# Two more projections of a decoder layer multiplied as pairs of chunks: the recurrent branch's input and the second half of the last gate

## The chip, the cores and the metric

The kernel runs on one core of a Trainium2 chip. The metric is the device time of one execution in microseconds (us); several executions give a median. A profiled execution gives the trace, on which the span runs from the first instruction to the last. The engines are named as in the profile: PE multiplies matrices (PEld loads its stationary operand), DVE is the vector engine, ACT the scalar engine, POOL is GpSimd, SP issues most of the transfers.

## The reference, cut to what matters

One decoder layer for 256 tokens of width 2048 in float32. One wide projection feeds three branches, each of 1024 channels: block attention (A), sliding-window attention (B), and a convolution with a gated linear recurrence (C). The layer ends in an output projection and a per-layer gate.

```python
h = rmsnorm(x, norm_g)
proj = h @ w_in                      # split into qa, ka, va, ga, qb, kb, vb, gb, xc, gc, mg
ya = moba_attention(qa, ka, va, ...)
yb = swa_attention(qb, kb, vb, ...)
yc = rglru_branch(xc, ...)
y_d = einsum(stack([ya * silu(ga), yb * silu(gb), yc * silu(gc)]), w_br)
merged = sum of sigmoid(mg) * y_d over the three branches
x = x + merged @ w_out
x = x + sigmoid(rmsnorm(x, ple_norm_g) @ w_pg) * (p @ w_pp)
return rmsnorm(x, final_norm_g)
```

Two products matter here: xc, which is h times a 2048 x 1024 slice of w_in, and x times w_pg, the last gate (2048 x 2048), of which the second 1024 columns are changed.

## The kernel before, in words

**Float32 from three products.** A float32 operand is split into a high part (an ACT copy with rounding, L141, or L139 where the sign is turned) and the remainder (a DVE subtraction, L147 or L145). `mm3` (L194) multiplies high by high, high by low and low by high into the same PSUM bank. A weight tile is 128 x 1024, two blocks of 512 columns. It is fetched by SP into one of six raw buffers (`fetch`, L104), split into one of four pairs of split buffers (`split`, L120), and then feeds 12 matmuls: two k-tiles, two halves of 128 tokens, three products. The splits are emitted 100 places ahead in priority (LEAD).

**Chunks and pairs.** A chunk is 512 output columns over 16 k-tiles: `project` (L228) runs it in eight weight tiles. `pair_of` (L264) computes two chunks together. For the first four k-tiles it treats tokens, k-tiles and chunks as 2 x 2 blocks and forms the result from seven block products (named `seven`, `one`, `six`, `five`, `three`, `two`, `four`) instead of eight; each is 6 matmuls on a weight tile of its own. The operand sums on the activation side come from `make_sums` (L248), once for each input; those on the weight side are tiles called `chain` and `lone` in a block `b_...`. SP loads a row of weights into each (L391) and POOL adds another row on top in an accumulating transfer (L275); further terms are added in the same way or on DVE, which the argument `adds` chooses. Four products, the heads, are queued in `coming` and run between the weight tiles of whatever comes before the pair; `head` (L204) decides when, counting the tiles that are left. Their partial sums z are copied out of PSUM, summed and, for chunk 0, placed as the start of the pair's own PSUM tile, on which everything else accumulates. `rest` (L359) then runs the remaining twelve k-tiles, six tiles for each chunk, with `three`, `two` and `four` after turns 0, 2 and 4. With `inside` set, the heads accumulate in the pair's own PSUM tile; there are two such tiles of two banks and four single banks (`aux`).

**Order of the work.** PE works through the projections in the order of the code: va (two chunks), xc (two chunks), then the pairs gc, qa, ka, ga and so on. A tile scheduler orders the instructions of every engine by priority and by data. What is not matrix work is paced by hand: at each weight tile a `tick` (L155) pops one step from the lists `side` and `todo`, and timers set with `later` run after a number of ticks. Branch C's gates are such steps (`gates_of`, L729, four for each of eight blocks); the scan and what follows are popped from `side` while ka and ga are computed (L1033). The operand sums of h are made while the first chunk of xc is multiplied (hook at k-tile 8, L783).

A result chunk is turned to feature order (`to_features`, L697): ACT scales it out of PSUM, DVE transposes 32 x 32 blocks, and SP writes it to HBM and reads it back (`flip`, L870), four transfers and one. Ten ticks later (`SETTLE`) `place` (L765) copies it to where the convolution reads it.

**The last gate.** Its chunks 0 and 1 are interleaved (L1217) so that the last four k-tiles, whose input comes last, are multiplied at the end. Chunk 2 follows as one chunk. Chunk 3 is run in three passes over weights that are kept: 48 matmuls of 512 columns for tokens 0 to 127, then two passes of 48 with 256 columns each for the other tokens, so that little work is left behind the last matmul. Each piece goes through `output` (L1181): sigmoid, times the parked product, plus x, square sum, and a multiplication by the final weights (L1188); `store` scales by the final norm and writes out.

There are 14 blocks of 128 x 2048 (`block`), and four buffers of 128 x 1024 for short use (`temp`).

Of the kernel before, what the change touches and what calls it, by code (L numbers as in the profile page):

```python
# [16 lines left out]
P = 128  # L17
# [31 lines left out]
SETTLE = 10  # L49
RV = 384  # L50
# [4 lines left out]
def trunk(ctx: ExitStack, tc: tile.TileContext, x, early, table, onehot, maskv, w_in, sinks, conv, w_ri, vec, fin, w_br,  # L55
# [138 lines left out]
    def mm3(ps, a, b, first, last, **more):  # L194
        (ah, al), (bh, bl) = a, b
        nc.tensor.matmul(ps, ah, bh, start=first, stop=False, **more)  # L196
        nc.tensor.matmul(ps, ah, bl, start=False, stop=False, **more)  # L197
        nc.tensor.matmul(ps, al, bh, start=False, stop=last, **more)  # L198
# [65 lines left out]
    def pair_of(act, sums, src, row, name, inside=False, adds=4, early=1):  # L264
# [29 lines left out]
        def product(n, a, r, dst, start=False, stop=False):  # L294
            w = split(f"{name}_m{n}", r, n == 1)
            for q in range(2):
                mm3(dst, a(q), [t[:, q * CW : (q + 1) * CW] for t in w], q == 0 and start, q == 1 and stop,
                    skip_group_check=True)
# [41 lines left out]
        def two():  # L340
            pss.append(matrix_psum(f"{name}_1"))
            for h in range(NH):
                place(pss[1][:, h], z[h])
            r = raw_of(3)
            with tc.issue_after(banks[1]):
                product(2, whole(1, 0), r, pss[1][:, 0])
# [3 lines left out]
        def four():  # L350
            product(4, whole(1, 1), chain, pss[1][:, 1])
            tick()
# [6 lines left out]
        def rest(ends, done, at_turn=(0, 2, 4), then=None):  # L359
# [4 lines left out]
            def usual(i, k0):  # L364
# [5 lines left out]
                for k in range(k0, k0 + WT // CW):  # L370
                    c = slice((k - k0) * CW, (k - k0 + 1) * CW)
                    for h in range(NH):
                        mm3(pss[i][:, h], [t[:, h * P : (h + 1) * P] for t in act()[k]], [t[:, c] for t in w], False,
                            k == KD - 1, skip_group_check=True)

            turns = [(i, k) for a, b in zip((PAIRED,) + ends, ends) for i in range(2) for k in range(a, b, WT // CW)]
            for n, (i, k) in enumerate(turns):
# [6 lines left out]
                if then is not None and n == THEN:  # L384
                    then()

# [210 lines left out]
    def in_pair(before, inside=False, early=1, adds=4):  # L597
        r = row_no[0] + before * KD * CW // WT
        coming, rest = pair_of(lambda: h_act, lambda: sums["h"], w_in, r, f"in{r}", inside, adds, early)

        def finish(done, then=None):
# [82 lines left out]
    first_ps = in_chunk(hooks={14: tables})  # L684
    works = [lambda c=c: squares(c) for c in range(4)] + [norm_rows, bias_rows]
    second_ps = in_chunk(hooks={2 * i: f for i, f in enumerate(works)})
# [37 lines left out]
    def branch_c():  # L724
# [36 lines left out]
        def turned_xc(c, ps):  # L761
# [9 lines left out]

            later(SETTLE, place)

# [14 lines left out]
        gs = [temp(f"gc{c}").rearrange("p k t -> p (k t)") for c in range(2)]  # L788
        gc_pair(lambda c, ps: to_features(gs[c], ps, rs1, f"gc{c}"), qa[0][0])
# [36 lines left out]
        steps += [(lambda c: split_act(z, 4 * c, 4, flipped(gs[c], 8), "zc"), c) for c in range(2)]  # L826
# [43 lines left out]
    def flip(dst, srcs, n, name, queue=nc.sync):  # L870
# [9 lines left out]
        queue.dma_start(dst, d)  # L880
# [145 lines left out]
    def branch_a(rest, qa_pair):  # L1026
# [3 lines left out]
        def turned_k(c, ps):  # L1030
            to_features(chunk(kT, c), ps, rs1, f"ka{c}")
            if c == 0:
                side.extend([lambda: None] * 4 + rest)  # L1033
# [32 lines left out]
    def turn_later(u, n, src, name, gain=None, ticks=TURN_LATE):  # L1066
# [15 lines left out]
        if n == 0 and name == "m":  # L1082
            later(ticks + 1, lambda: sums_of(u, name))
# [89 lines left out]
    for n, (to, src) in enumerate(rows):  # L1173
        later(2 + n, lambda to=to, src=src: nc.scalar.dma_start(to, src))
# [34 lines left out]

    def gated(n, ps):  # L1210
# [5 lines left out]
    gets = [weights_of(w_pg, i * KD * CW // WT, f"pg{i}", WT // CW) for i in range(2)]  # L1216
    for last in (False, True):  # L1217
# [9 lines left out]
    gated(2, project(act_of(*x2T), w_pg, 2 * KD * CW // WT, "pg2"))  # L1227

    kept.update(f"pg3_{s}" for s in range(KD // 4))
    ws = weights_of(w_pg, 3 * KD * CW // WT, "pg3", WT // CW)  # L1230
    y, junk = token_major(temp("y3")), token_major(temp("jz3"))
    c0 = 3 * CW
    ps = project(act_of(*x2T), None, 0, "pg3", weights=ws, half=0)
    output(0, c0, CW, ps, y[:, 0, :], junk[:, 0, :], square_act(0, 3))()
# [4 lines left out]
    def part_of(c):  # L1239
        def get(k):  # L1240
            w, kk = ws(k)
            return [t[:, kk * CW + c * HW : kk * CW + (c + 1) * HW] for t in w], 0
        return get

    for c in range(2):
        ps = project(act_of(*x2T), None, 0, f"pg{3 + c}", cw=HW, weights=part_of(c), half=1)[:, :HW]
# [31 lines left out]
def _pack_pair(w, ends=(KD,)):  # L1278
# [3 lines left out]
    for lo, hi in zip((PAIRED,) + ends, ends):  # L1282
        for t in (a, b):
# [4 lines left out]
def _columns_of(w, paired):  # L1288
    parts, at = [], 0
    for width, pair in paired:  # L1290
        c = w[:, at : at + width]
        at += width
        parts += [_pack_pair(c[:, i : i + 2 * CW]) for i in range(0, width, 2 * CW)] if pair else [_pack(c)]
# [64 lines left out]
```

## Time and profile before

| | |
|---|---|
| median of 3 runs | 979.05 us (978.0 to 981.14) |
| the profiled execution's own time | 977.16 us |
| its span | 975.1 us |
| matmuls | 4390, PE busy 965.5 us |
| DVE, ACT busy | 721.8 us, 620.9 us |
| transfers | 255.71 MB, mean 262 GB/s |

How to read the rows: a row of the timeline has the start in us from the span's start, the duration in us, the engine (a q behind it is its queue, which issues transfers), the line of the code, the operation, output<-inputs, the shape, and in brackets the idle time before it and what ended it. A row of a group has busy us and mean ns of one behind the bar. PE's matmuls overlap, so the distance between two starts tells more than a duration.

### The profile page before, as it was taken

The numbers are of one execution on the slowest core, as the hardware profiler recorded it, in microseconds if no ns is written. First come the engines' busy times: TensorE is split into PE (matmuls) and PEld (weight loads), VectorE is DVE, ScalarE is ACT, GpSimd is POOL, SyncE is SP. The second block draws the span as 40 slices with busy tenths as digits, with TensorE's granted clock in tenths as the row PEclk, the third lists the DMA queues.
The fourth block names the chain that finished last, engine by engine and source line by source line (L and its number), as shares of the span: only waits on it lengthen the run. The fifth ranks groups of instructions, "written<-read, shape, count | busy, mean of one in ns | idle before, by whom it ended". The sixth has DMA issues, their size and how long they took to land.

```text
span 975.1 us, 12612 instructions
## 1 busy us (share of the span) xinstructions
PE 965.5 (99%) x4390; PEld 804.3 (82%) x4390; DVE 721.8 (74%) x1005; ACT 620.9 (64%) x881; POOL 33.1 (3%) x45
## 2 busy tenths in 40 slices
PE   9999999999999999999999999999999999999996
PEld 7888888888888888888888888888888888888886
DVE  6855898866897676667677788788578587765673
ACT  7654776667777666556566866765566565665652
POOL 0010000010000000000000000000000000000000
PEclk9999999999999999999999999999999999999999
DMA  9978989799989865897787876776978998788742
GB/s 342 352 236 253 328 270 340 249 308 281 305 266 321 257 219 189 249 280 244 237 282 245 286 230 225 231 227 208 303 203 280 301 297 305 254 278 334 233 151 87
DMA packets 90264, 255.71 MB, mean 262 GB/s; under 512 B 10152, under 2 KB 31704, under 8 KB 90072
## 3 DMA queue, kind: packets, MB, share of 16 engines
q1 hardware_dynamic: 72720, 216.69, 64.4%
q0 software_dynamic: 4752, 17.30, 9.8%
q10 hardware_dynamic: 12728, 20.91, 6.4%
q8 instruction: 34, 0.56, 0.2%
q14 instruction: 30, 0.25, 0.1%
HBM read 234.13 MB, written 20.75 MB: 261 GB/s over the span
## 4 chain that ended last, share of the span: by engine, by line
PE 98%; DMA 0%; DVE 0%; ACT 0%; SPq 0%; issue 0%; DVEq 0%; ACTq 0%
PE ps_in L197 21%; PE ps_in L196 20%; PE ps_in L198 20%; PE ps_pg L198 3%; PE ps_pg L196 3%; PE ps_pg L197 3%; PE ps_out L196 3%; PE ps_out L198 3%; PE ps_out L197 3%; PE ps_bra L197 1%; PE ps_bra L196 1%; PE ps_brc L197 1%; PE ps_brc L198 1%; PE ps_brc L196 1%; PE ps_brb L197 1%; PE ps_brb L196 1%
## 5 line engine op out<-in xcount | busy, mean ns | idle before, releaser
L147 DVE TENSOR_TENSOR wl_in<-r_in,wh_in 128x1024 fp32r<-128x1024 f32 x196 | 239.0, 1222 | 95.6 <-ACT wh_in L141 91.3
L197 PE MATMUL ps_in<-wl_in,h 128*128 128x512 f32 x784 | 305.6, 390 | 0.4 <-DVE wl_in L147 0.4
L196 PE MATMUL ps_in<-wh_in,h 128*128 128x512 f32 x784 | 305.6, 390 | 0.0
L198 PE MATMUL ps_in<-wh_in,h 128*128 128x512 f32 x784 | 305.3, 389 | 0.0
L141 ACT CAST wh_in<-r_in 128x1024 fp32r<-128x1024 f32 x196 | 205.3, 1051 | 141.3 <-PE ps_in L198 105.1
L197 PEld LDWEIGHTS ps_in<-wl_in,h 128*128 128x128 f32 x784 | 147.3, 188 | 30.4 <-DVE wl_in L147 0.8
L198 PEld LDWEIGHTS ps_in<-wh_in,h 128*128 128x128 f32 x784 | 147.2, 188 | 30.4
L196 PEld LDWEIGHTS ps_in<-wh_in,h 128*128 128x128 f32 x784 | 147.2, 188 | 30.0
L147 DVE TENSOR_TENSOR wl_in_m<-b_in,wh_in_m 128x1024 fp32r<-128x1024 f32 x36 | 43.9, 1220 | 22.7 <-ACT wh_in_m L141 22.2
L147 DVE TENSOR_TENSOR wl_pg<-r_pg,wh_pg 128x1024 fp32r<-128x1024 f32 x28 | 33.9, 1222 | 27.4 <-ACT wh_pg L141 26.6
L141 ACT CAST wh_in_m<-b_in 128x1024 fp32r<-128x1024 f32 x36 | 37.8, 1049 | 25.0 <-PE ps_in L198 13.1
L275 POOL DMA_DIRECT2D b_in<-w_in_dram x29 | 25.5, 878 | 638.6 <-DMA b_in<-w_in_dram 395.7
L196 PE MATMUL ps_pg<-wh_pg,x_hi 128*128 128x512 f32 (+1 forms) x120 | 45.0, 375 | 0.0
L197 PE MATMUL ps_pg<-wl_pg,x_hi 128*128 128x512 f32 (+1 forms) x120 | 45.0, 375 | 0.0
L198 PE MATMUL ps_pg<-wh_pg,x_lo 128*128 128x512 f32 (+1 forms) x120 | 45.0, 375 | 0.0
L141 ACT CAST wh_pg<-r_pg 128x1024 fp32r<-128x1024 f32 x28 | 29.1, 1049 | 22.1 <-PE ps_pg L198 17.3
L196 PE MATMUL ps_out<-wh_out,m_hi 128*128 128x512 f32 x96 | 37.3, 389 | 0.0
L197 PE MATMUL ps_out<-wl_out,m_hi 128*128 128x512 f32 x96 | 37.3, 389 | 0.0
L198 PE MATMUL ps_out<-wh_out,m_lo 128*128 128x512 f32 x96 | 37.3, 389 | 0.0
L147 DVE TENSOR_TENSOR wl_out<-r_out,wh_out 128x1024 fp32r<-128x1024 f32 x24 | 29.1, 1220 | 10.2 <-ACT wh_out L141 10.2
L141 ACT CAST wh_out<-r_out 128x1024 fp32r<-128x1024 f32 x24 | 25.2, 1050 | 12.5 <-PE ps_out L198 8.1
L141 ACT CAST wh_brb<-r_brb 128x1024 fp32r<-128x1024 f32 x16 | 16.9, 1053 | 20.6 <-PE ps_brb L198 10.9
(360 smaller groups left out, 1638.3 us busy)
## 6 DMA issues: line engine op xcount, KB each, us to landing
r_in<-w_in_dram SPq DMA_DIRECT2D x223, 512.0 KB, 4.9
r_pg<-w_pg_dram SPq DMA_DIRECT2D x32, 512.0 KB, 4.8
r_out<-w_out_dram SPq DMA_DIRECT2D x30, 512.0 KB, 5.0
b_in<-w_in_dram POOLq DMA_DIRECT2D x29, 512.0 KB, 8.4
b_in<-w_in_dram SPq DMA_DIRECT2D x18, 512.0 KB, 5.3
r_brc<-w_br_dram SPq DMA_DIRECT2D x16, 512.0 KB, 6.3
r_bra<-w_br_dram SPq DMA_DIRECT2D x16, 512.0 KB, 4.3
r_brb<-w_br_dram SPq DMA_DIRECT2D x16, 512.0 KB, 6.3
```

The lines of the kernel that those rows point to most:

```text
L141: casts.append(nc.scalar.copy(hi[:, c], r[:, c]).ins)
L147: los.append(nc.vector.tensor_tensor(lo[:, c], r[:, c], of, op=ALU.subtract).ins)
L196: nc.tensor.matmul(ps, ah, bh, start=first, stop=False, **more)
L197: nc.tensor.matmul(ps, ah, bl, start=False, stop=False, **more)
L198: nc.tensor.matmul(ps, al, bh, start=False, stop=last, **more)
L275: nc.gpsimd.dma_start(t, src[row + i], accum_op=ALU.add)
```

## The change

1. *xc becomes a pair* with a new order (`late`): its second chunk is multiplied first. Its PSUM tiles start from the ordinary k-tiles; the partial sums z are added to them in PSUM by DVE at the end of each chunk (`finish`). The seven products are run at turns 2, 3, 4, 5, 7, 8 and 9 of its twelve (`XC_AT`). It is opened at k-tile 9 of the second chunk of va, and the sums of h are made at k-tile 12 of that chunk.
2. *The pair gc* is opened at turn 6 of xc and no longer runs its heads in its own PSUM tile; the pair qa is prepared at turn 11. The steps behind get other distances: `place` after 13 ticks instead of 10, two more empty steps ahead of the scan's list, three ahead of each part of the result's split.
3. *Chunks 2 and 3 of the last gate become a pair* (`parts`), opened while chunk 0 is multiplied; its heads run between the tiles of chunks 0 and 1. Chunk 3's part of the first four k-tiles is placed in three single banks (half 0, and two of 256 columns), and product `four` is split into two of 256 columns. The three passes then cover the remaining twelve k-tiles. The sums of that input are made twelve ticks after its first quarter is there.
4. The parked products and final weights are loaded from tick 10 on instead of 2. The multiplications by the final weights for chunks 0 to 2 move into chunk 3's first pass (`weighing`).

The weights are packed in the order that this needs. The core of the diff:

```diff
+SUMS_LATE = 12
+PARKED_LATE = 10
+OPEN_AT = (0, 8)
+XC_AT = (2, 3, 4, 5, 7, 8, 9)
...
         def five():
             product(5, sum_of(0), lone, banks[0], stop=True)
             place(z[2], banks[0])
+            if late:
+                z[3] = lone[:, CW:]
+                banks[1] = on_vector(z[3], z[2], banks[7], ALU.add)
+                return
             if not inside:
...
         def two():
-            pss.append(matrix_psum(f"{name}_1"))
-            for h in range(NH):
-                place(pss[1][:, h], z[h])
+            if parts:
+                pss.append([aux(f"ps_{name}_{c}") for c in range(3)])
+                place(pss[1][0], z[0])
+                for c, t in enumerate(pss[1][1:]):
+                    place(t[:, :QW], z[1][:, c * QW : (c + 1) * QW])
+            elif not late:
+                pss.append(matrix_psum(f"{name}_1"))
+                for h in range(NH):
+                    place(pss[1][:, h], z[h])
...
+        def turned_over(usual, done, then):
+            pss[:] = [None, matrix_psum(f"{name}_1")]
+            turns = [(i, k) for i in (1, 0) for k in range(PAIRED, KD, WT // CW)]
+            steps = heads[:4] + [three, two, four]
+
+            def finish(i):
+                for h in range(NH):
+                    on_vector(pss[i][:, h], pss[i][:, h], z[2 * (1 - i) + h], ALU.add)
+                done(i, pss[i])
+
+            for n, (i, k) in enumerate(turns):
+                if n == KD // 4 + 2:
+                    pss[0] = matrix_psum(f"{name}_0")
+                if i == 0:
+                    head(len(turns) - n)
+                for _ in range(late.count(n)):
+                    steps.pop(0)()
+                usual(i, k)
+                if not steps and n == late[-1]:
+                    finish(1)
+                if n in then:
+                    then[n]()
+            finish(0)
...
+    def prepare_xc():
+        xc_pair.append(in_pair(0, adds=2, late=XC_AT)[1])
+
-    second_ps = in_chunk(hooks={2 * i: f for i, f in enumerate(works)})
+    second_ps = in_chunk(hooks={2 * i: f for i, f in enumerate(works)} | {9: prepare_xc, 12: sum_h})
...
-            later(SETTLE, place)
+            later(SETTLE + 3, place)
...
-        for c in range(2):
-            if c:
-                open_gc, gc_pair = in_pair(1, True)
-                open_gc()
-            turned_xc(c, in_chunk(hooks={14: prepare} if c else {8: sum_h}))
+        def prepare_gc():
+            gc.append(in_pair(0))
+            gc[0][0]()
+
+        xc_pair[0](turned_xc, {6: prepare_gc, 11: prepare})
+        gc_pair = gc[0][1]
...
-        later(2 + n, lambda to=to, src=src: nc.scalar.dma_start(to, src))
+        later(PARKED_LATE + n, lambda to=to, src=src: nc.scalar.dma_start(to, src))
...
-            output(h, n * CW, CW, ps[:, h, :], y[:, h, :], junk[:, h, :], square_act(h, n))()
+            weighing.append(output(h, n * CW, CW, ps[:, h, :], y[:, h, :], junk[:, h, :], square_act(h, n)))
...
+                if (i, k) == OPEN_AT:
+                    open_pair, pair = pair_of(lambda: act_of(*x2T), lambda: sums["x2"], w_pg, row, "pg2", early=0, parts=True)
+                    open_pair()
+                if (i, k) in ((1, KD - 6), (0, KD - 4), (0, KD - 2), (1, KD - 4)):
+                    coming.pop(0)()
...
-    gated(2, project(act_of(*x2T), w_pg, 2 * KD * CW // WT, "pg2"))
+    pss = pair((KD,), lambda i, ps: gated(2, ps), chunks=range(1))
...
+    def products(at, h, c, n):
+        for k in range(KD - PAIRED):
+            w, kk = ws(k)
+            if weighing and n == CW and kk:
+                weighing.pop(0)()
+            ends[at] = mm3(pss[1][at][:, :n], [t[:, h * P : (h + 1) * P] for t in act_of(*x2T)[PAIRED + k]],
+                [t[:, kk * CW + c : kk * CW + c + n] for t in w], False, k == KD - PAIRED - 1, skip_group_check=True)
+        return pss[1][at][:, :n]
```

More of the change, by code (lines that the diff above doesn't have):

```diff
@@ L197, in mm3 @@
         nc.tensor.matmul(ps, ah, bl, start=False, stop=False, **more)
-        nc.tensor.matmul(ps, al, bh, start=False, stop=last, **more)
+        return nc.tensor.matmul(ps, al, bh, start=False, stop=last, **more).ins
     coming = []
@@ L262, in make_sums, with pair_of @@
         return parts
-    def pair_of(act, sums, src, row, name, inside=False, adds=4, early=1):
+    def pair_of(act, sums, src, row, name, inside=False, adds=4, early=1, parts=False, late=()):
         names = ("11", "12", "22", "21")
@@ L350, in four @@
         def four():
-            product(4, whole(1, 1), chain, pss[1][:, 1])
+            if parts:
+                product(4, whole(1, 1), chain, [t[:, :QW] for t in pss[1][1:]])
+            else:
+                product(4, whole(1, 1), chain, pss[1][:, 1])
             tick()
@@ L357, in pair_of, with rest @@
         heads = [seven, one, six, five] + [settle] * early
-        def rest(ends, done, at_turn=(0, 2, 4), then=None):
+        def turned_over(usual, done, then):
[19 more added lines that the diff above has]
+            finish(0)
+        def rest(ends, done, at_turn=(0, 2, 4), then=None, chunks=range(2)):
             while coming and coming[0] in heads:
@@ L372, in usual @@
                     for h in range(NH):
-                        mm3(pss[i][:, h], [t[:, h * P : (h + 1) * P] for t in act()[k]], [t[:, c] for t in w], False,
-                            k == KD - 1, skip_group_check=True)
-            turns = [(i, k) for a, b in zip((PAIRED,) + ends, ends) for i in range(2) for k in range(a, b, WT // CW)]
+                        mm3(pss[i][:, h], [t[:, h * P : (h + 1) * P] for t in act()[k]], [t[:, c] for t in w],
+                            bool(late) and k == PAIRED, k == KD - 1, skip_group_check=True)
+            if late:
+                return turned_over(usual, done, then)
+            turns = [(i, k) for a, b in zip((PAIRED,) + ends, ends) for i in chunks for k in range(a, b, WT // CW)]
             for n, (i, k) in enumerate(turns):
@@ L595, in trunk, with in_pair, finish @@
     sums = {}
-    def in_pair(before, inside=False, early=1, adds=4):
+    def in_pair(before, inside=False, early=1, adds=4, late=()):
         r = row_no[0] + before * KD * CW // WT
-        coming, rest = pair_of(lambda: h_act, lambda: sums["h"], w_in, r, f"in{r}", inside, adds, early)
-        def finish(done, then=None):
+        coming, rest = pair_of(lambda: h_act, lambda: sums["h"], w_in, r, f"in{r}", inside, adds, early, late=late)
+        def finish(done, then={} if late else None):
             row_no[0] += 2 * KD * CW // WT
@@ L1032, in turned_k @@
             if c == 0:
[L1033 removed]
+                side.extend([lambda: None] * 6 + rest)
         following.pop(0)(turned_k, begin_next)
@@ L1081, in turn_later @@
         later(ticks, finish)
-        if n == 0 and name == "m":
-            later(ticks + 1, lambda: sums_of(u, name))
+        if n == 0:
+            later(ticks + (1 if name == "m" else SUMS_LATE), lambda: sums_of(u, name))
     def merge(z, bi, br):
@@ L1292, in _columns_of @@
         at += width
-        parts += [_pack_pair(c[:, i : i + 2 * CW]) for i in range(0, width, 2 * CW)] if pair else [_pack(c)]
+        parts += [_pack_pair(c[:, i : i + 2 * CW], late=pair > 1) for i in range(0, width, 2 * CW)] if pair else [_pack(c)]
     return np.concatenate(parts)
```

60 lines of the change are left out of this document (38 added, 22 removed).

## The prediction

> **What bounds the kernel now.** I read the page first: its busy shares, its slices and its chain.
>
> ```profile
> span 975.1 us, 12612 instructions
> PE 965.5 (99%) x4390; PEld 804.3 (82%) x4390; DVE 721.8 (74%) x1005; ACT 620.9 (64%) x881; POOL 33.1 (3%) x45
> ...
> PE   9999999999999999999999999999999999999996
> DVE  6855898866897676667677788788578587765673
> ...
> PE 98%; DMA 0%; DVE 0%; ACT 0%; SPq 0%; issue 0%; DVEq 0%; ACTq 0%
> ```
>
> The chain that ended last is 98% matmuls, and no slice but the last shows PE under 9 tenths. So a matmul less is worth its pitch, as long as nothing new makes PE wait; everything on another engine is free until then. The pitch is not the 389 ns that one matmul lasts, because they overlap. The timeline of PE gives it, from first and last rows:
>
> ```profile
> 61.65 0.39 PE L196 MATMUL ps_in<-wh_in,h 128*128 128x512 f32 x1
> 83.41 0.39 PE L196 MATMUL ps_in<-wh_in,h 128*128 128x512 f32 x1
> ...
> 88.84 0.39 PE L196 MATMUL m_in<-wh_in_m,sum_h 128*128 128x512 f32 x1
> 90.20 0.39 PE L196 MATMUL ps_in<-wh_in,h 128*128 128x512 f32 x1
> ...
> 955.35 0.28 PE L196 MATMUL ps_pg<-wk_pg,x_hi 128*128 128x256 f32 x1
> 961.10 0.28 PE L196 MATMUL ps_pg<-wk_pg,x_hi 128*128 128x256 f32 x1
> ```
>
> The first chunk of the recurrent projection is 96 matmuls from 61.65 to 83.41: 226.7 ns each, 2.72 us for a weight tile of 12. A product of a pair is 6 matmuls in 1.36 us, the same pitch. A half pass of the last gate, with 256 columns, is 48 matmuls in 5.75 us: 119.8 ns each.
>
> How near the other engines are to making PE wait is read in the busy time by stretch (columns: window, its length, then PE, PEld, DVE, ACT, POOL, the clock, the DMA share, GB/s) and in the timeline of ACT and DVE:
>
> ```profile
> 61.00:108.00 47.00, 47.00 (x209) 38.93 (x208) 28.63 (x29) 26.00 (x31) 3.96 (x5) 1.00 0.92 282
> 108.00:150.00 42.00, 42.00 (x195) 35.03 (x194) 36.72 (x76) 29.93 (x44) 3.20 (x4) 1.00 0.94 294
> 193.00:236.00 43.00, 43.00 (x195) 35.75 (x194) 29.05 (x29) 27.24 (x34) 3.49 (x4) 1.00 0.94 291
> 236.00:278.00 42.00, 42.00 (x187) 34.78 (x186) 36.12 (x37) 34.57 (x40) 3.47 (x4) 1.00 0.97 301
> 889.00:911.00 22.00, 22.00 (x99) 18.22 (x98) 12.51 (x13) 12.48 (x15) 0.71 (x1) 1.00 0.88 333
> ...
> 80.89 1.05 ACT L141 CAST wh_in_m<-b_in 128x1024 fp32r<-128x1024 f32 x1 [1.67 <-PE ps_in L198]
> ...
> 283.38 1.22 DVE L147 TENSOR_TENSOR wl_in<-r_in,wh_in 128x1024 fp32r<-128x1024 f32 x1
> 284.52 1.22 DVE L416 TENSOR_TENSOR zc_lo<-gc,zc_hi 128x1024 fp32r<-128x1024 f32 x1
> 285.65 1.22 DVE L147 TENSOR_TENSOR wl_in_m<-r_in,wh_in_m 128x1024 fp32r<-128x1024 f32 x1
> ```
>
> The cast at 80.89 feeds the product whose first matmul is the row at 88.84: 7.95 us ahead, and it had waited 1.67 us for PE to free one of the four split buffers. In this stage the splits are as far ahead as the buffers let them be. DVE is 61% busy there, 87% in the next stretch and back to back near 284, yet PE is busy the whole of each stretch: DVE at 87% has been carried without a stall.
>
> **The change, part by part.** *Fewer matmuls.* The recurrent projection (xc) has 2 chunks x 16 k-tiles x 2 halves x 3 = 192 matmuls. As a pair it has 7 products x 6 = 42, and 2 x 12 x 2 x 3 = 144 for the other twelve k-tiles: 186. Six less at 226.7 ns: **-1.36 us**. The last two chunks of the gate have 96 + 48 matmuls of 512 columns and 96 of 256. Afterwards there are 36 for six products, 72 for the third chunk's rest and 36 for half 0: again 144 of 512; and 12 for product four plus 72 in the two half passes: 84 of 256. Twelve less at 119.8 ns: **-1.44 us**. Together **-2.80 us**, all on the path.
>
> On this the Trainium skill (TensorE: Matmul & The Clock Gate, Back-to-back issue gap) has columns/2.4 + 2.5 ns for a warm matmul, 216 and 109 ns here, by which the sum would be 2.60 us (an estimate from that page); the rows, 226.7 and 119.8, decide.
>
> *More splits and sums beside them.* Each new pair splits three more weight tiles and adds these:
>
> ```profile
> L147 DVE TENSOR_TENSOR wl_in<-r_in,wh_in 128x1024 fp32r<-128x1024 f32 x196 | 239.0, 1222 | 95.6 <-ACT wh_in L141 91.3
> L141 ACT CAST wh_in<-r_in 128x1024 fp32r<-128x1024 f32 x196 | 205.3, 1051 | 141.3 <-PE ps_in L198 105.1
> L279 DVE TENSOR_TENSOR b_in<-b_in,r_in 128x1024 f32<-128x1024 f32 x7 | 8.6, 1223 | 3.4 <-DMA r_in<-w_in_dram 3.3
> L279 DVE TENSOR_TENSOR ps_in<-b_in,m_in 128x512 f32<-128x512 f32 x9 | 6.2, 694 | 2.5 <-ACT b_in L284 2.1 <-ACT ps_in L284 0.4
> L284 ACT COPY ps_in<-z_in 128x512 f32<-128x512 f32 x18 | 10.6, 589 | 0.3
> L875 DVE STREAM_TRANSPOSE flip_qa<-qa 128x1024 f32<-128x1024 f32 x2 | 2.5, 1246 | 0.0
> 84.56 1.26 ACT L702 ACTIVATE xc<-ps_in,rs_in 128x512 f32<-128x512 f32 x2
> ```
>
> For xc on DVE: 3 x 1.22, two chain sums of 1.22, a subtraction and an addition of 0.69, the four closing sums in PSUM at 0.69, and one transpose of 1.25 that lay in the next stage: 3.66 + 2.44 + 1.38 + 2.76 + 1.25 = 11.5 us, so 28.6 + 11.5 = 40.1 of 47 us, 85%. That is below the 87% that the next stretch carries. The dense place is turns 7 to 9, where three products of xc and four of its neighbour (gc) share three turns: 7 x 1.36 + 3 x 2.72 = 17.7 us of PE against ten splits (12.2), one chain sum, one subtraction and two closing sums, 15.5 us of DVE. It fits, with 2 us over; the tightest split is that of turn 7, with 3 x 1.36 us between the freeing of its buffer and its use, less 2.3 for cast and remainder: 1.8 us of slack. Cost zero; 1.5 us if DVE comes there with the whole of another transpose and chain sum in front.
>
> *The closing sums.* gc is no longer computed inside its own PSUM tile, because xc holds both; its sum has to wait until chunk 1 of xc is read out. After xc's product four that is 2 x 0.69 on DVE, 1.26 on ACT, a copy of 0.59 and a sum of 0.69: 3.9 us, against the turns 9, 10 and 11 of PE, 8.2 us. Zero; queued behind are only splits, which have 1.8 us or more.
>
> *Loads and queues.* A pair's chain is a load from SP and an accumulating one from POOL on top:
>
> ```profile
> b_in<-w_in_dram POOLq DMA_DIRECT2D x29, 512.0 KB, 8.4
> b_in<-w_in_dram SPq DMA_DIRECT2D x18, 512.0 KB, 5.3
> ...
> 41.92 1.06 ACT L141 CAST wh_in<-r_in 128x1024 fp32r<-128x1024 f32 x1 [0.71 <-PE ps_in L198]
> 54.06 1.64 POOL L450 TENSOR_TENSOR rs_in<-rs_in,half_c 128x2 f32<-128x2 f32 x1 [44.33 <-DVE rs_in L449]
> 64.61 0.91 SPq L391 DMA_DIRECT2D b_in<-w_in_dram  x2
> 101.98 0.91 SPq L391 DMA_DIRECT2D b_in<-w_in_dram  x2
> ```
>
> With the split (2.3 us) a chain needs 5.3 + 8.4 + 2.3 = 16.0 us before its first matmul. xc's is opened behind the cast at 41.92, so at about 43; its first matmul is two turns after 61.65, near 67: 24 us. On POOL the two accumulating loads come ahead of the row at 54.06; they wait for loads that land near 49, so it isn't held. gc's chain, now at 64.61, 24 us before 88.84, is opened at xc's turn 6, one turn before use; but SP fetches six raw tiles ahead. The fetch in front of it stands level with turn 1, and from there to gc's first product are 6 x 2.72 + 4 x 1.36 = 21.8 us of PE, and the split lead on top. Zero, as long as that holds (second rival). The two transposed copies of xc come near each other on SP, which the fetch-ahead covers.
>
> *What moves later.* The steps of the recurrent gates start some 25 us later and so run into 193 to 236, where DVE is 68% busy; two of eight blocks, about 7 us of DVE, make it 84%. Zero. In the last gate, the operand sums (some 4 us of DVE) and three splits fall where DVE is 57% busy (889 to 911). The loads that move ten ticks back still go out several tiles before they are read. Zero.
>
> *The tail.* Six multiplications by the final weights move into the last full pass, now 36 x 226.7 ns = 8.2 us.
>
> ```profile
> L1188 DVE TENSOR_TENSOR xr<-xr,fg 128x512 f32<-128x512 f32 (+1 forms) x8 | 5.0, 654 | 1.6 <-ACT jz L1191 1.6
> 955.55 0.69 ACT L1184 ACTIVATE y<-ps_pg,rs 128x512 f32<-128x512 f32 x1 [3.80 <-PE ps_pg L198]
> 963.05 0.19 ACT L1191 ACTIVATION_READ_ACCUMULATOR jz<-xr 128x1 f32 x1
> 967.06 0.47 ACT L1184 ACTIVATE y<-ps_pg,rs 128x256 f32<-128x256 f32 x1 [3.82 <-PE ps_pg L198]
> ```
>
> That is 4.1 us, beside four steps of 0.69 for the third chunk and one or two splits: 8.1 to 9.3 us. From half 0 (955.55) to the end of the first half pass (963.05, and some 0.9 on DVE) the side work takes 8.4 us; the two half passes leave it 11.5 now and 72 x 119.8 ns = 8.6 afterwards. So zero to 0.6 us; I take zero, since the first four multiplications need nothing of that pass.
>
> The sum against the profiled execution's own time is 977.16 - 2.80 = 974.4 us. It lay 1.9 us under the median of 979.05, so in terms of the median: **976.3 us**.
>
> **Rivals.** *First: DVE is crowded.* For it: splits with little slack at turn 7 and back-to-back work near 284, where the steps now end two ticks later. Against: the stretches at 87% without a stall. Its price is 1.5 us at turn 7, or the 0.6 of the tail, or both: 977.0 to 978.4, say 977.7, no measurable difference.
>
> *Second, slower: gc's chain comes late.* If SP sends its loads only when turn 6 is split, as those at 101.98 sit behind a cast, they go out 7.95 + 2.72 = 10.7 us ahead of gc's first product where 16.0 are needed. PE waits 5.3 us there. The load that is then accumulated on the same chain for product six (8.4, and 2.3 for its split) starts with no lead left, 10.7 us against the 3 x 1.36 + 2.72 = 6.8 us of PE between the two products, so PE waits another 3.9 us, and the kernel ends at 976.3 + 9.2 = 985.5 us. It decides from the point where the lead falls below 16.0 us, and the gain is gone when 2.8 us are waited. For it: with xc's own, all 14 blocks of the pool are taken, and a late release holds the loads. Against: this opening stands in no hook and depends on a fetch alone. The same delay would come if accumulating loads took longer:
>
> ```profile
> L275 POOL DMA_DIRECT2D b_in<-w_in_dram x29: 865/868/1046, 69.4 to 718.9; - x29
> ```
>
> Minimum, median and maximum of an issue lie within 0.2 us, whatever DVE does. The Trainium skill (DMA: Bandwidth & Descriptors, SWDGE vs HWDGE vs iDMA) says that DVE in its two-port mode locks GpSimd out of the descriptor rings, which speaks against more such loads; these 29 issues show no sign of it.
>
> **How the numbers follow.** About 0.3%, 2.9 us, is what can be told from no change here. My sum of 2.8 lies just inside, and a median of such runs moves by half a microsecond to one (three of them spread from 978.0 to 981.14). Forecast, 0.72: 976.3, give or take 1.2 for the two medians, 975.1 to 977.5; the bound of 976.1 cuts it a little below its middle, so 0.35 of it lies beyond the bound and 0.37 within. Crowded DVE, 0.17: 0.15 within it and 0.01 beyond either end by the spread of the medians. Late chain, 0.11: slower. So faster 0.36, same 0.52, slower 0.12. The range takes in the forecast with both ends of its median and the crowded case with both its prices; the late chain is left out: 974.8 to 979.0.
>
> **What would show it.** PE with 4372 matmuls instead of 4390; no PE row with idle time before it near 86 (gc's first product), at turn 7, or where gc begins; the cast of gc's first product waiting for PE and not for b_in; the last half passes 36 matmuls each, the first step of the third output 8.6 us after half 0's. A PE row that waits for wl or b_in there, or a last slice that grows, proves me wrong.

## The result, and the profile after

The changed kernel takes **985.09 us** (median of 6 runs, 983.52 to 986.79) where the kernel before took 978.35 (6 runs, 977.19 to 981.14): ratio 1.0064, 95% interval 1.0049 to 1.008. It is slower by about 6.7 us where 2.8 less were forecast, and the time lies outside the forecast's range of 974.8 to 979.0. The profiled execution took 985.03 us.

First the page of the changed kernel:

```profile
span 983.2 us, 12645 instructions
PE 966.3 (98%) x4372; PEld 802.7 (82%) x4372; DVE 738.2 (75%) x1027; ACT 631.9 (64%) x899; POOL 37.6 (4%) x51
...
PE   9999999999999999999999999999999999999896
...
PEclk9999999999999999999999999999999999999898
...
PE 5%; DMA 1%; DVE 0%; ACT 0%; issue 0%; DVEq 0%; ACTq 0%
```

The 18 matmuls are gone (4372), and ahead of the tail one slice of PE falls under 9 tenths, the third from the end (910 to 934), where the clock does so too. The chain that ended last was 98% PE before; now it can be followed back only to a transfer that was issued at 911.55, through some 7% of the span. The account starts from there.

Where the time lies is read from PE's first rows of each stage. At the first row of the gate (878.59, before 879.19) the changed kernel is 0.60 us ahead. From there to the end of the last matmul it takes 96.17 us where it took 87.83 and should take 1.44 less, 86.39. The tail behind the last matmul grew from 8.10 to 8.49. So 8.3 us were lost inside the last gate. PE's rows there show two places:

```profile
900.12 0.39 PE L203 MATMUL ps_pg<-wh_pg,x_lo 128*128 128x512 f32 x1
902.09 0.49 PE L201 MATMUL ps_pg<-wh_pg,x_hi 128*128 128x512 f32 x1 [1.59 <-ACT wh_pg L146]
903.35 0.50 PE L202 MATMUL ps_pg<-wl_pg,x_hi 128*128 128x512 f32 x1 [0.76 <-DVE wl_pg L152]
...
919.45 0.39 PE L203 MATMUL ps_pg<-wh_pg,x_lo 128*128 128x512 f32 x1
923.76 0.79 PE L201 MATMUL ps_pg<-wh_pg,x_hi 128*128 128x512 f32 x1 [3.92 <-ACT wh_pg L146]
924.35 0.70 PE L201 MATMUL m_pg<-wh_pg_m,sum_x 128*128 128x512 f32 x1
```

From start to start, less the pitch of 0.23: the first wait is 1.75 + 1.03 + 0.11 = 2.9 us, the second 4.08 + 0.36 + 0.27 = 4.7 us. Behind the second, some ten matmuls come 427 ns apart instead of 227, another 2.0 us; from 925.0 to 929.3 the granted clock was 0.52. Together 9.6 us, of the 96.17 - 86.39 = 9.8 to be explained. Both waits are for ACT's cast of an ordinary weight tile, so the next view is ACT's timeline, with its queue, of the changed kernel:

```profile
887.50 2.20 ACTq L942 DMA_DIRECT2D d_x<-flip_x  x2
889.80 2.00 ACT L146 CAST wh_pg<-r_pg 128x1024 fp32r<-128x1024 f32 x2 [1.27 <-PE ps_pg L203]
900.53 0.34 ACTq L946 DMA_DIRECT2D turn_x<-d_x  x1
901.00 1.99 ACT L146 CAST wh_pg<-r_pg 128x1024 fp32r<-128x1024 f32 x2 [9.20 <-DMA r_pg<-w_pg_dram]
...
908.46 1.04 ACT L146 CAST wh_pg_m<-b_pg 128x1024 fp32r<-128x1024 f32 x1
...
921.72 1.04 ACT L146 CAST wh_pg_m<-b_pg 128x1024 fp32r<-128x1024 f32 x1 [8.94 <-DMA fg<-fin_dram]
922.67 1.04 ACT L146 CAST wh_pg<-r_pg 128x1024 fp32r<-128x1024 f32 x1
```

and the same in the kernel before:

```profile
888.75 1.34 ACTq L879 DMA_DIRECT2D d_x<-flip_x  x2
890.13 0.48 ACTq L1174 DMA_DIRECT2D fg<-fin_dram  x1
...
895.60 0.33 ACTq L880 DMA_DIRECT2D turn_x<-d_x  x1
896.05 2.00 ACT L141 CAST wh_pg<-r_pg 128x1024 fp32r<-128x1024 f32 x2 [3.03 <-PE ps_pg L198]
```

ACT issues the four writes of the transposed copy (d_x) and then the read back (turn_x), which waits for them. That shows in the landing of the last write: in the changed kernel it came 12.2 us after the issue at 888.25, and the read back went out 0.1 us later; in the kernel before 5.9 us after the issue at 889.57, and again the read back 0.1 us later. ACT takes its work in order: while its queue stands at the read back, no split behind it starts (here the cast comes 0.47 us behind it, in the third experiment and both probes below 0.46 or 0.47). From the end of the last write's issue to the read back 5.5 us passed before (890.09 to 895.60) and 10.8 us after (889.70 to 900.53). In both kernels ACT made two more splits in that time; then it was idle for 3.0 us before and 9.2 us after. The idle time in brackets names the load of r_pg. That load was no cause: the cast's tile, asked for at 881.99, had landed by 887.53 by the trace's semaphore counts. The second hole ends with product six's cast (921.72); the ordinary tile's cast is queued behind it. The chain of waits of the changed kernel names the releaser:

```profile
911.55 10.07 DMA b_pg<-w_pg_dram
...
922.67 1.05 ACT wh_pg L146
923.72 0.04 issue
923.76 0.79 PE ps_pg L201
```

This is the accumulating load that adds to the tile `chain` between product seven, cast at 908.46, and product six. (The brackets at 921.72 name the load of fg, which nothing there reads.)

The engine time and the traffic around the first hole, before and after (columns as in the prediction: the last two are the DMA share and GB/s):

```profile
884.00:902.00 18.00, 18.00 (x81) 14.92 (x80) 12.35 (x14) 8.49 (x11) 0.71 (x1) 1.00 1.00 388
```

```profile
884.00:902.00 18.00, 16.51 (x73) 13.33 (x71) 9.36 (x13) 6.34 (x10) 2.43 (x3) 1.00 0.92 281
888.00:892.00 4.00, 4.00 (x20) 3.30 (x19) 2.35 (x2) 2.53 (x3) 0.68 (x1) 1.00 0.97 217
```

In 888 to 892, while the four writes run, the DMA engines are busy at 0.97 but move 217 GB/s. The kernel before moves 341 at a share of 0.93 in the same four us, and 388 at 1.00 over the 18 us. The two accumulating loads that open the gate's pair were issued just ahead, by POOL:

```profile
885.61 0.86 POOL L280 DMA_DIRECT2D b_pg<-w_pg_dram  x1 [102.80 <-DVE wl_pg L152]
886.89 0.86 POOL L280 DMA_DIRECT2D b_pg<-w_pg_dram  x1 [0.42 <-issue]
```

### The profile page after: what moved, and what is told of

Its sections match the earlier page's. It is cut to its first block, busy times and chain, and to the rows that moved or that the text cites. A ratio compares the mean times of both kernels' runs of the same rounds, so it can differ in the third digit from the quotient of the medians.

```text
span 983.2 us, 12645 instructions
## 1 busy us (share of the span) xinstructions
PE 966.3 (98%) x4372; PEld 802.7 (82%) x4372; DVE 738.2 (75%) x1027; ACT 631.9 (64%) x899; POOL 37.6 (4%) x51
## 5 line engine op out<-in xcount | busy, mean ns | idle before, releaser
L202 PE MATMUL ps_in<-wl_in,h 128*128 128x512 f32 x768 | 299.7, 390 | 0.4 <-DVE wl_in L152 0.4
L201 PE MATMUL ps_in<-wh_in,h 128*128 128x512 f32 x768 | 299.4, 390 | 0.0
L203 PE MATMUL ps_in<-wh_in,h 128*128 128x512 f32 x768 | 299.3, 390 | 0.0
L152 DVE TENSOR_TENSOR wl_in<-r_in,wh_in 128x1024 fp32r<-128x1024 f32 x192 | 233.8, 1220 | 87.0 <-ACT wh_in L146 83.7
L146 ACT CAST wh_in<-r_in 128x1024 fp32r<-128x1024 f32 x192 | 201.2, 1051 | 136.0 <-PE ps_in L203 110.0
L202 PEld LDWEIGHTS ps_in<-wl_in,h 128*128 128x128 f32 x768 | 144.2, 188 | 30.1 <-DVE wl_in L152 0.8
L203 PEld LDWEIGHTS ps_in<-wh_in,h 128*128 128x128 f32 x768 | 144.2, 188 | 29.8
L201 PEld LDWEIGHTS ps_in<-wh_in,h 128*128 128x128 f32 x768 | 144.2, 188 | 29.6
L152 DVE TENSOR_TENSOR wl_in_m<-b_in,wh_in_m 128x1024 fp32r<-128x1024 f32 x40 | 48.8, 1221 | 24.4 <-ACT wh_in_m L146 23.7
L146 ACT CAST wh_in_m<-b_in 128x1024 fp32r<-128x1024 f32 x40 | 42.0, 1050 | 26.9 <-PE ps_in L203 17.6
L152 DVE TENSOR_TENSOR wl_pg<-r_pg,wh_pg 128x1024 fp32r<-128x1024 f32 x26 | 31.5, 1220 | 24.3 <-ACT wh_pg L146 24.3
L203 PE MATMUL ps_pg<-wh_pg,x_lo 128*128 128x512 f32 (+1 forms) x112 | 42.3, 378 | 0.0
```

The lines of the kernel that those rows point to most:

```text
L146: casts.append(nc.scalar.copy(hi[:, c], r[:, c]).ins)
L152: los.append(nc.vector.tensor_tensor(lo[:, c], r[:, c], of, op=ALU.subtract).ins)
L203: return nc.tensor.matmul(ps, al, bh, start=False, stop=last, **more).ins
```

## The experiments

**Theory one** is read from these rows: the accumulating loads of the gate's pair do the harm. The two that open it run on top of the transposed copy and hold ACT's queue; the one between seven and six has too little lead. Its rivals: the recurrent projection has a share in it; the products of the pair stand too close; it is the added bytes, whatever the kind of transfer; the parked loads, moved by ten ticks, collide with them.

**1. The recurrent projection alone.** The gate, its sums and its parked loads go back to how they were:

```diff
-PARKED_LATE = 10
+PARKED_LATE = 2
-    pss = pair((KD,), lambda i, ps: gated(2, ps), chunks=range(1))
+    gated(2, project(act_of(*x2T), w_pg, 2 * KD * CW // WT, "pg2"))
```

> The recurrent projection as a pair alone, the last gate as it was. Theory one (all of the loss lies in the gate's pair) expects the kernel before less 6 matmuls of 0.227 us: about 1.3 us under it, 977.0 us, and no PE row of w_in with idle time before it. Rival (the crowded turns 7 to 9 or the moved gate steps cost something too): 978 to 979 us.

Measured: 977.63 us (976.6 to 978.84), ratio 0.9988 (0.9977 to 1.0), some 1.2 us less, close to the 1.36 of six matmuls, though the interval just reaches no change. No wait shows in its gate, so no loss is seen in this part.

**2. The gate alone.**

```diff
-    second_ps = in_chunk(hooks={2 * i: f for i, f in enumerate(works)} | {9: prepare_xc, 12: sum_h})
+    second_ps = in_chunk(hooks={2 * i: f for i, f in enumerate(works)})
-    parts = [(va, BW, 0), (xc, BW, 2), (gc, BW, 1), (qa, BW, 1), (ka, BW, 1), (ga, BW, 1), (mg + 2 * D, D, 1),
+    parts = [(va, BW, 0), (xc, BW, 0), (gc, BW, 1), (qa, BW, 1), (ka, BW, 1), (ga, BW, 1), (mg + 2 * D, D, 1),
```

> The last gate's pair alone, the recurrent projection as it was. Theory one expects the whole loss here: 985.1 + 1.3 = 986.4 us, with the same two waits of PE as in the changed kernel, about 2.9 us near 900 and 4.4 us near 920, and the lower clock behind the second. If the two pairs disturb each other: under 984 us.

Measured in one execution: 988.36 us, with both waits (3.63 + 1.03 + 0.22 at 902.62 and 2.31 + 0.27 + 0.35 at 925.33), each with slow matmuls behind it. The first wait is longer than expected and the second shorter; the loss is the gate's.

**3. The later sums on DVE.** The opening keeps its two accumulating loads, the two later ones are replaced by DVE additions:

```diff
-                    open_pair, pair = pair_of(lambda: act_of(*x2T), lambda: sums["x2"], w_pg, row, "pg2", early=0, parts=True)
+                    open_pair, pair = pair_of(lambda: act_of(*x2T), lambda: sums["x2"], w_pg, row, "pg2", early=0, adds=2, parts=True)
```

> The changed kernel with the gate's chain updated on DVE from rows that are fetched anyway (as xc's is); the two accumulating loads of the opening stay. Theory one (the chain's accumulating load is what product six waits for) expects the second wait and the low clock behind it to go, 985.1 - 4.4 - 2.3 = 978.4 us, and the first wait near 900 to stay. Rival (the heads stand too near each other, whoever adds): the wait before product six stays at 2 us or more and the time over 982 us.

Measured: 982.71 us, ratio 1.0039 (1.0025 to 1.0053). The second wait is gone, as theory one says. The first was larger than I expected (2.71 + 1.03 + 0.36 at 902.12, and this time slow matmuls behind it too), so the time was missed by 4 us.

**4. No accumulating load in the gate.** In addition the opening rows are loaded plainly and added on DVE:

```diff
+                if parts:
+                    fetch(src, row + i, f"{name}_open{i}")
+                    on_vector(t, t, raws.pop(f"{name}_open{i}")[0], ALU.add)
+                else:
+                    add_to(t, i)
```

> As the one before, and the opening's two sums too are made from plain loads and DVE additions, so the gate's pair has no accumulating load at all; bytes loaded are the same. Theory one (the opening's accumulating loads hold up the transposed copy of x, for which ACT's queue stands) expects both waits to go: 985.1 - 9.6 = 975.5 us. Rival (the copy is held up by the amount of traffic, whatever its kind): the wait near 900 stays and the time is about 978.4 us.

Measured: 977.8 us (975.83 to 979.69), ratio 0.999 (0.9976 to 1.0005). Both waits are gone, as theory one says, but the time is 2.3 us above its forecast, and no gain over the kernel before is shown. (The rival's 978.4 is nearer, but the wait that it keeps is gone.) ACT's queue in the third and then in this fourth experiment:

```profile
890.20 1.78 ACTq L942 DMA_DIRECT2D d_x<-flip_x  x2
903.49 0.34 ACTq L946 DMA_DIRECT2D turn_x<-d_x  x1
```

```profile
888.41 2.27 ACTq L946 DMA_DIRECT2D d_x<-flip_x  x4
896.23 0.34 ACTq L950 DMA_DIRECT2D turn_x<-d_x  x1
```

The read back stands 11.5 us behind the writes with the accumulating opening and 5.6 us with as many bytes loaded plainly. So it is not the number of bytes. Left over were 0.84 us at 890 and 0.65 us at 907 to 912, where DVE's additions stood in front of splits.

**5. The parked loads back at tick 2,** and nothing else:

```diff
-PARKED_LATE = 10
+PARKED_LATE = 2
```

> The changed kernel with the parked loads back at tick 2 instead of 10, nothing else. Theory one (the accumulating loads hold up the transposed copy of x, and product six's chain lands too late): the six parked loads then compete with the transposed copy near 889, so the first wait (2.9 us) stays or grows by 1 to 2 us; they are gone from the stretch where product six waits, and that wait (4.1 us and some 2 us of slow matmuls behind it) shrinks by at most the engine time of two loads, 2.9 us. Together 983 to 986 us. Rival (the parked loads are what delays product six's chain): the second wait vanishes with what stands behind it, 979 us.

Measured in one execution: 977.67 us. **Theory one did not forecast this.** Every accumulating load is still there, and both waits are gone. The rival's number, 979, was nearer, but its reason would have left the first wait. SP's timeline in the changed kernel, and then SP's and POOL's in this one, show why:

```profile
876.49 1.46 SPq L117 DMA_DIRECT2D r_pg<-w_pg_dram  x2
878.05 0.86 SPq L439 DMA_DIRECT2D b_pg<-w_pg_dram  x2
```

```profile
877.74 6.00 SPq L117 DMA_DIRECT2D r_pg<-w_pg_dram  x3
883.84 1.25 SPq L439 DMA_DIRECT2D b_pg<-w_pg_dram  x2
...
894.74 0.90 POOL L280 DMA_DIRECT2D b_pg<-w_pg_dram  x1 [4.63 <-PE ps_pg L203]
896.16 0.86 POOL L280 DMA_DIRECT2D b_pg<-w_pg_dram  x1 [0.52 <-issue]
```

The scheduler now puts one more weight tile in front of the pair's first loads on SP, and that tile must wait for its buffer until 883.42. So the pair's loads go out 5.8 us later, and they take longer to land (10.2 and 11.0 us instead of 6.9 and 7.8). POOL's accumulating loads, which come 0.6 to 0.7 us behind these landings, go out at 894.74 and 896.16 instead of 885.61 and 886.89: behind the issue of the four writes, no longer beside it. The read back is issued 4.7 us behind the writes. (The issue of the writes itself took longer here, so from the first write's issue to the read back the gain is smaller: 11.1 us instead of 13.9.)

This execution came to the gate 2.0 us later (first row at 880.59 instead of 878.59), so its times are better counted from there. The read back comes 18.5 us into the gate instead of 21.9. Six's accumulating load starts 26.3 us into it (906.84) instead of 33.0 (911.55). Of these 6.7 us, 2.9 are the first wait, which PE no longer makes; the other 3.8, with a landing in 9.6 instead of 10.1 us, are 4.2 of the 4.7 us that PE had waited for six. Both waits hang on where the accumulating loads fall, and the parked loads set that.

**6. Product six later,** with all accumulating loads kept:

```diff
-                if (i, k) in ((1, KD - 6), (0, KD - 4), (0, KD - 2), (1, KD - 4)):
+                if (i, k) in ((1, KD - 6), (0, KD - 4), (1, KD - 4), (1, KD - 2)):
```

> The changed kernel with products six and five two weight tiles (5.4 us) later, all accumulating loads kept. Theory one: an accumulating load lands some 10 us after its issue, so 5.4 us more cover the 4.1 us that PE waited for product six; the second wait is gone with the slow matmuls behind it (6.7 us together), the first (2.9 us) stays: 978.4 us. Rival (the DMA engines are simply full there, so that the wait only moves): 2 us or more of it come back at product six's new place or at the tile before it, 981 to 985 us.

This edit moves six by one tile, 2.72 us, not by two as the expectation says. Measured in one execution: 987.75 us. The second wait fell from 4.7 to 2.2 us (1.53 + 0.54 + 0.12), about that one tile. The first stayed (2.3 us). But five now stood directly ahead of the pair's other k-tiles, and a new wait of 3.7 us came behind it at 934.30, for the sums that follow five. More spacing pays for the load and is charged at the other end.

**7. The opening later,** after the third experiment's edit:

```diff
-OPEN_AT = (0, 8)
+OPEN_AT = (1, 2)
-                if (i, k) in ((1, KD - 6), (0, KD - 4), (0, KD - 2), (1, KD - 4)):
+                if (i, k) in ((0, KD - 4), (0, KD - 2), (1, KD - 4), (1, KD - 2)):
```

> The changed kernel with the further sums of the gate's pair on DVE, and its opening, still with two accumulating loads, five weight tiles later, product seven one tile later. Theory one: no accumulating load runs beside the four writes of the transposed copy any more, so ACT's queue is held by them for about 6.4 us as without such loads, and the first wait is gone: 977 to 978.5 us, unless seven's chain itself comes late (it has some 2 us over). Rival (the writes are held by something else of the change, for instance the earlier rush of raw tiles): ACT's queue is held for 12 us again and PE waits 3 to 4 us: 982 us.

Measured in one execution: 985.55 us; the time was missed by 7 us. The time that the writes hold the read back was as theory one says: with the accumulating loads at 902.6 and 903.8, the read back came 4.8 us behind the writes (887.99 to 892.78). But 2.0 us of waits stayed between 900 and 905, where ACT now stood 3.7 us at its first step on the copy that was read back (898.00). The chain of seven, 10.11 us from issue to landing, was now late as well (1.6 us at 913.24), and five, again directly ahead of the rest, cost 3.7 us and slow matmuls at 932.20. This run shows how long the writes hold the read back, not a better kernel.

**8. The sums on DVE at their own places.** As in the fourth, but the opening of `chain` is added without the splits' priority, and `lone` from the tile that product one loads anyway:

```diff
+            if parts:
+                nc.vector.tensor_tensor(lone, lone, r, op=ALU.add)
...
+            if parts:
+                fetch(src, row + 2, f"{name}_open")
+                nc.vector.tensor_tensor(chain, chain, raws.pop(f"{name}_open")[0], op=ALU.add)
```

> Both pairs, without any accumulating load in the gate: chain's opening sum on DVE at its own place in the program instead of ahead of the splits, lone's from the tile that product one loads anyway, behind that product. Theory one: the waits that were left with all sums on DVE ahead of the splits (0.84 us at 890, 0.65 us at 907 to 912) came from these sums standing in front of the splits; they go, and the kernel takes 977.8 - 1.4 = 976.4 us, about 0.2% under the kernel before. Rival (DVE has no room there wherever the sums stand): a wait of 1 us or more at another place, 977.5 us or more.

Measured: 978.53 us (975.7 to 982.65, 12 runs) beside 979.71 for the kernel before; ratio 0.9995 (0.9981 to 1.001). In the profile the waits of the gate fell from 1.5 to 0.75 us (at 902.69 and 906.05); this execution was the fastest of the twelve, 975.7 us. The times decide neither way.

**9 and 10. Two probes.** These have the recurrent projection as a pair and the gate as before (they compute all that the kernel before does), with the parked loads at tick 10. Where the gate's pair would be opened, a block that nothing reads is loaded, in the one with accumulation, in the other without:

```diff
+                if (i, k) == OPEN_AT:
+                    t = block("b_probe")
+                    with tc.issue_after(loads[-1]):
+                        for j in range(2):
+                            part = t[:, j * WT : (j + 1) * WT]
+                            nc.sync.dma_start(part, w_pg[KD + 1])
+                            nc.gpsimd.dma_start(part, w_pg[KD + 2 * j], accum_op=ALU.add)
```

> The recurrent projection as a pair, the gate as before, with the parked loads at tick 10, and in the place where the gate's pair would be opened two loads by SP and two accumulating loads by POOL into a block that nothing reads. It computes what the kernel before does. Theory one (it is the accumulating loads, running while the transposed copy is written, that hold ACT's queue): the read back is issued about 12 us after the last of the four writes, ACT makes no split meanwhile, and PE waits 2 to 4 us near 900: 979 to 982 us. Rival (the pair's products, sums or order do it): the read back about 6 us behind, no wait, 977 us.

> The same as the probe with two accumulating loads, but POOL's two loads overwrite the block instead of being added to it: the same queue, bytes and places, without the accumulation. Theory one: these occupy the DMA engines no longer than other loads, the read back is issued 6 to 8 us after the last write, and PE waits less than 0.5 us: 977 to 977.5 us. Rival (POOL's queue or the added bytes do it, whatever the loads do): 12 us and 2 to 4 us of waiting as in the other probe.

Measured in one execution each: **984.79 us** with accumulation, **976.6 us** without. Two accumulating loads whose sum is never used lie 8.2 us above the same two from the same queue, overwriting, which make PE wait nowhere in the gate. (The accumulating probe came out 3 us above its expectation, because its first wait was 5.5 us, and 2.0 us of slow matmuls followed.) ACT and PE in the accumulating probe:

```profile
888.14 2.91 ACTq L942 DMA_DIRECT2D d_x<-flip_x  x2
902.85 0.34 ACTq L946 DMA_DIRECT2D turn_x<-d_x  x1
```

```profile
900.12 0.39 PE L203 MATMUL ps_pg<-wh_pg,x_lo 128*128 128x512 f32 x1
904.41 0.50 PE L201 MATMUL ps_pg<-wh_pg,x_hi 128*128 128x512 f32 x1 [3.90 <-ACT wh_pg L146]
```

and ACT in the plain one:

```profile
887.03 1.34 ACTq L942 DMA_DIRECT2D d_x<-flip_x  x2
896.96 0.34 ACTq L946 DMA_DIRECT2D turn_x<-d_x  x1
```

In every run with this wait, PE's next matmul starts 1.56 us after the read back's issue: 904.41 - 902.85 here, 902.09 - 900.53 in the changed kernel, 905.05 - 903.49 in the third experiment. So the end of the wait is set by the read back alone. PE ran out of split tiles at 900.35 in the changed kernel and in this probe, so it waits when the read back is issued later than 900.35 - 1.56 = 898.8. The plain probe needs the tile at 900.19 and has 1.7 us in hand, though its read back too came 8.6 us behind the writes.

The queues between 884 and 902 (packets, MB, share of 16 engines), with accumulation and without:

```profile
q1 hardware_dynamic: 983, 3.56, 52.4%
q0 software_dynamic: 288, 1.05, 31.6%
```

```profile
q1 hardware_dynamic: 942, 3.42, 51.5%
...
q0 software_dynamic: 288, 1.05, 17.7%
```

For the same 1.05 MB and 288 packets the accumulating loads held the engines 31.6% of 18 us, 5.7 us, and the overwriting ones 3.2 us: 1.8 times as long for a byte. The other queue takes the same for a byte in both (2.65 and 2.71 us per MB).

**11. The parked loads at tick 2, timed** (the edit of experiment 5).

> The changed kernel with the parked loads back at tick 2, now timed. Theory one, as it stands after the single look at it: the parked loads push the pair's first loads back by some 6 us, so that its two accumulating loads no longer run on top of the four writes of the transposed copy; ACT is not held, product seven is cast in time and product six with it. No wait of PE is left but some 0.3 us: two times the saved matmuls, 2.8 us, less 0.3 and 0.4 for a longer tail, 2.1 us under the kernel before, ratio 0.998. Rival (the single look was luck, the order of these loads differs from run to run): times spread up to 985 us, ratio 1.000 or more.

Measured: 977.3 us (976.24 to 978.89) beside 979.44 for the kernel before; ratio **0.9978** (0.9967 to 0.9989). The order of the loads is as in experiment 5: POOL's openings at 894.87 and 896.11, the read back at 899.08, 4.6 us behind the writes. One wait of 1.2 us is left in the gate, at 893.67; there the issue of the first two writes took ACT's queue 4.85 us.

**12. Both:** the parked loads at tick 2 and the sums of experiment 8.

> The parked loads at tick 2 and no accumulating load in the gate, the sums on DVE at their own places. Theory one: neither wait has a cause left; waits of 0.3 us at most in the gate, 2.1 to 2.4 us under the kernel before, ratio 0.9977. Rival (with the parked loads early there is nothing left for the sums on DVE to gain, and they crowd the splits): the same as or slower than the one with the parked loads alone, ratio 0.999.

Measured: **976.3 us** (975.67 to 977.06), ratio **0.9968** (0.9958 to 0.9978): faster than the kernel before by some 3 us, and by the two ratios (0.9968 and 1.0064) faster than the changed kernel. Against experiment 11 it is 0.1% apart, with intervals that overlap; the profile speaks for it, since the 1.2 us of waits are gone as well. From its page:

```profile
PE 963.6 (99%) x4372; PEld 801.5 (82%) x4372; DVE 743.0 (76%) x1031; ACT 632.2 (65%) x899; POOL 34.4 (4%) x47
```

PE has no wait of even 0.1 us left in the gate.

## Why the prediction was wrong

*Fewer matmuls, -2.80 us:* right. The count is 4372, and the version without the waits gains 0.32%, 3.1 us.

*More work on DVE beside xc, zero:* right, with the load put too high. The stretches of the changed kernel:

```profile
61.00:108.00 47.00, 47.00 (x209) 38.95 (x208) 32.92 (x32) 29.98 (x36) 5.29 (x6) 1.00 0.93 273
...
193.00:236.00 43.00, 43.00 (x200) 35.73 (x199) 35.56 (x46) 29.96 (x42) 3.48 (x4) 1.00 0.94 281
```

DVE is 70% busy in the first, where I had worked out 85%; where the other 7 us of its steps went was not followed up. In 193 to 236 it is 83%, as worked out (84%). PE is busy throughout both.

*gc's chain in time:* right. Its cast stands in ACT's timeline with PE as what it waited for, 6.6 us ahead of the product's first matmul at 86.24:

```profile
79.64 1.05 ACT L146 CAST wh_in_m<-b_in 128x1024 fp32r<-128x1024 f32 x1 [0.96 <-PE ps_in L203]
```

*What moves later, in the last gate: "The loads that move ten ticks back still go out several tiles before they are read. Zero." This step failed.* It asked whether the moved loads come in time for their own readers, and they did. It did not ask what goes out in the place they leave. One constant, `PARKED_LATE`, is the difference between 985.09 and 977.3 us (ratios 1.0064 and 0.9978 to the kernel before): with the parked loads gone, the pair's first loads go out 5.8 us sooner, POOL's accumulating loads run on top of the transposed copy, and PE waits 2.9 and 4.7 us. It takes both. With the parked loads late and no accumulating load in the gate (experiment 4), or with the parked loads early and the accumulating ones kept (experiment 11), neither of the two waits appears.

*Loads and queues: also incomplete.* I weighed the lead of a chain for xc and for gc, and for the gate's own pair not at all. Its four accumulating loads have no term in the sum. The view of the kernel before would have warned: between 884 and 902 the DMA engines are at a share of 1.00. So would my own figures: 16.0 us of lead are needed before a chain's first matmul, and for six's load 8.4 and 2.3 from the product before it. In the changed kernel it took 10.07 us to land.

*The late-chain rival (985.5 us)* met the number and half of the mechanism. It forecast an accumulating load for product six that starts without lead, which is the second wait. But it put it at gc instead of the gate, and the first wait is no late chain: it is ACT, held by the transposed copy. That the figure agrees is chance.

*The tail, zero to 0.6, taken as zero:* it grew by 0.39 us. In the changed kernel the third output's first step comes 974.79 - 966.17 = 8.6 us after half 0's, as worked out:

```profile
966.17 0.69 ACT L1250 ACTIVATE y<-ps_pg,rs 128x512 f32<-128x512 f32 x1
...
974.79 0.47 ACT L1250 ACTIVATE y<-ps_pg,rs 128x256 f32<-128x256 f32 x1 [1.45 <-PE ps_pg L203]
```

The account of the loss, on the profiled executions (the 9.8 and the 0.4 are read from the result, not derived): 0.60 ahead at the start of the gate, 1.44 saved and 9.8 lost inside it, 0.4 in the tail: 977.16 - 0.60 - 1.44 + 9.8 + 0.4 = 985.3; measured 985.03.

*What stays open.* Why 2.5 us more of engine time (5.7 less 3.2) become 4.8 us more from the first write's issue to the read back (887.23 to 902.85 with accumulation, 15.6 us; 886.17 to 896.96 without, 10.8 us): how the engines share their time between queues no run here shows. The two probes were executed once each. Nor did I trace why the scheduler puts one more weight tile ahead of the pair's first loads when the parked ones come early. And xc: at the start of the gate the changed kernel was 0.60 us ahead instead of 1.36; the rest lies in pieces too small to place.

## What to carry to other kernels

When a load is moved, ask two things: whether it still arrives in time, and which transfers now go out in its place and on top of what. ACT, which here both issues the round trip through memory and makes the splits, stood at the read back until the last write had landed, and every split behind it waited: keep accumulating loads off the DMA engines while such a round trip is under way. Overwriting loads of the same bytes did no harm there. Where DVE has room, a plain load and a DVE addition are worth more than an accumulating load at a place where the DMA engines are full.

## What the runs showed of the hardware

An accumulating load held the DMA engines 1.8 times as long as an overwriting load of the same bytes from the same queue (31.6% against 17.7% of 18 us), and landed 10.1 us after its issue at a place where the engines were full. The Trainium skill (DMA: Bandwidth & Descriptors, Rules for kernel authors) says that an accumulate reads its destination and writes it later; the longer engine time agrees with that, while the price of it is this case's own.

After 3.9 us of idle time PE ran ten matmuls at 427 ns instead of 227, with a granted clock of 0.52 from 925.0 to 929.3, and the wait of 4 us thus cost 2 more. The Trainium skill (TensorE: Matmul & The Clock Gate, Wait — 56ns, not 53.3ns?) gives 426.7 ns for a cold matmul of 512 columns, and these rows agree. How long a wait must be for this is not settled by its length alone: after the first wait of the changed kernel, with 1.59 and 0.76 us of idle time, the granted clock stayed at 1.00, while in experiment 6 a wait with 1.37 and 0.26 us of it was followed by seven such matmuls, at a granted clock of 0.52 from 926.0 to 929.3.
